# Bidirectional GLA/pool hybrid block: weights one lead further ahead in the units, loads moved up, attention put later into r

## The chip, the cores and the metric

One NeuronCore of a Trainium2 chip runs the whole kernel in one launch. The metric is device time in microseconds (us), the median of several runs; the profile is of one further execution of the same program. The engines are TensorE (PE in the profile; PEld is its loading of weights), VectorE (DVE), ScalarE (ACT), GpSimd (POOL) and SyncE (SP), from whose one queue nearly all DMAs are issued, in the order of the program.

## The reference

One layer of a hybrid encoder on x of 1024 tokens by 1024 features, float32:

```python
h = rmsnorm(x, norm_mix[l])
proj = h @ w_in[l]
q, k, v, r, lr_f, lr_b, u, g_a, g_b = jnp.split(proj, split_points, axis=-1)
# widths 512, 512, 1024, 1024, 16, 16, 512, 1024, 1024
log_a_f = jax.nn.log_sigmoid(lr_f @ w_decay_up_fwd[l] + b_decay_fwd[l]) / 16    # and log_a_b
o = gla_chunked(q, k, v, log_a_f, True) + flipped gla_chunked(..., log_a_b, False)   # 4 heads
o = o * lax.rsqrt(jnp.mean(o * o, axis=-1, keepdims=True) + EPS)
o = o * gla_norm[l] * jax.nn.silu(r)
y_a = o @ w_branch_gla[l]
y_b = (grouped linear map of multiscale_pool(u)) * pool_scale[l]      # windows 2, 4, 8, 16
merged = jax.nn.sigmoid(g_a) * y_a + jax.nn.sigmoid(g_b) * y_b
x = x + merged @ w_out[l]
h2 = rmsnorm(x, norm_ffn[l])
gate, up = jnp.split(h2 @ w_ffn_in[l], 2, axis=-1)                    # 2816 each
x = x + (jax.nn.silu(gate) * up) @ w_ffn_out[l]
return rmsnorm(x, norm_final)
```

## The kernel before

**Products.** Every float32 operand is split into a high and a low part (`split_to`: a cast on ScalarE, L197, gives hi; a subtraction, L198, on VectorE or for weights on GpSimd, gives lo). A product is three matmuls (hi hi, hi lo, lo hi; `mm3`, with the matmul in L269). Matmuls are of 128 x 128 weights on 512 columns. Many of the projections are made in two-by-two blocks by a scheme with seven products instead of eight (p = 1 to 7), whose combined operands VectorE and GpSimd prepare.

**The order of work.** The program is written in the order in which TensorE is to run, and each engine runs its own instructions in the order written. Side work is woven in by `pump`, called after every `mm3` with 1 (a "pump" is three matmuls): it runs things put off, weights in the making (`pending`), jobs beside (`aside`, each job charging so many pumps, from `prepare_beside`), and generators at the side (`side`, from `begin(generator, delay in pumps)`, each `yield` saying how many pumps to wait). `finish_beside` runs out what remains of the jobs at that place.

**The stages**, in order:

1. Norms, transposition to feature-major hT, and the values of head 0 (`values`, called for t = 0 to 6 in steps of two); `low_rank_weights` at t == 4. Then v of head 0 and half of hT are stored (`flush` issues what `later` deferred).
2. The decays' low-rank product (lrT, cast in L962, subtraction in L963), then `project_qk`: q and k of head 0, whose weights come through `fetch` (issue the load of raw weights, L205), `prepare` and `take`, in the order of `order`. Beside it run `feature_jobs`: sums of blocks of hT on VectorE (hs, L588), cast to trh (L582) and its rest trl (L573). They charge `SUMS` pumps each. `first_unit` is called by `project_qk` at each half of q and k.
3. Sixteen units (`gate_units`): two for u, three for the q and k of heads 1 to 3, three for v, four each for the gates a and b. A unit makes two column blocks of 128 by seven products of 12 matmuls. Its raw weights (fraw, two loads of 512 KB in `Unit.load`, L850) are combined (`Unit.source`, fs, L858), cast (wh) and reduced (wl, on GpSimd). `gates_ahead.step()` does this for the next product in the sequence of all units; one step is called in the loop ahead of each product, and some are called ahead of the loop. The pool `wts` has six buffers for wh and wl, four for raw and fs; the pool `slots` has 39 buffers of 512 KB. At the side run `decays`, then `pooling`.
4. r: eight projections of 16 `mm3`s, 128 pumps in all, over h (hh, hl); half of hT is read back from `h_out`. At the side runs `attention(h)` for the four heads: keys transposed (kp, L833, cast to kt), states (kv), outputs (op), normalized in L822, transposed (tp, L1399) and gated with r. Beside it run `branch_jobs` and `output_jobs`, sums of weights of the two coming projections on GpSimd (wsum, L588), stored to `s_out` and `t_wo` (L569).
5. `project(BRANCH)` and the merged projection, each of seven products with pieces from `line`: `line_load` (wraw, L1032), `line_sums`, `line_make` (casts and splits of weights wh, wl and data dh, dl). `load_block` (ob, L1060) reads back gated attention outputs.
6. The feed-forward part, untouched by the change.

The three constants that the change meets are `AHEAD = 4`, `SLOTS = 39` and `READY = 2`.

Of the kernel before, what the change touches and what calls it, by code (L numbers as in the profile page):

```python
# [11 lines left out]
F32R = mybir.dt.float32r  # L12
# [8 lines left out]
KT = D // P  # L21
# [21 lines left out]
AHEAD = 4  # L43
# [8 lines left out]
def kernel(  # L52
# [20 lines left out]
    nc = tc.nc  # L73
# [17 lines left out]
    def name(s):  # L91
        count[0] += 1
        return f"{s}_{count[0]}"

    def slot(dtype=F32, shape=(2, HALF), s="slot"):
        return slots.tile([P, *shape], dtype, tag="slot", name=name(s))
# [13 lines left out]
    def as_f32(ap):  # L110
        return ap.bitcast(F32)
# [74 lines left out]
    def begin(gen, delay=0.0):  # L186
        side.append([gen, delay])
# [12 lines left out]
    def load(src, kts, c0, width):  # L200
        per = min(HALF // width, kts)
        tiles = []
        for k0 in range(0, kts, per):
            raw = wts.tile([P, per, width], F32, tag="raw", name=name("raw"), bufs=4)
            nc.sync.dma_start(  # L205
                raw[:, :, :],
                src[k0 * P : (k0 + per) * P, c0 : c0 + width].rearrange("(k p) c -> p k c", p=P),
            )
            tiles.append(raw)
        return tiles  # L210
# [30 lines left out]
    def fetch():  # L241
        src = next(order, None)
        if src is not None:
            loaded.append(load(*src))

    def prepare():
        if not loaded:
            fetch()
        if loaded:
            ready.append(Weights(loaded.pop(0)))  # L250

            credit[0] = -2.0
# [101 lines left out]
    def load_up(i, d, w):  # L354
        r = 2 * RANK * i + RANK * d
        nc.sync.dma_start(uraw[r : r + RANK, :, d, :], w[0].rearrange("r (h c) -> r h c", h=HEADS))
# [12 lines left out]
    hT = Activations("h")  # L369
# [7 lines left out]
    def norms(t0):  # L377
        for t in (t0, t0 + 1):
            norm_x(t)
            yield 2  # L380
# [13 lines left out]
    def low_rank_weights():  # L394
        for i in range(2):
            raw = lraw[:, 4 * i : 4 * i + 4, :]
            nc.scalar.copy(lw[i][:, :, :3, :], raw.unsqueeze(2).broadcast_to([P, 4, 3, 2 * RANK]))
            nc.vector.tensor_tensor(lw[i][:, :, 3, :], raw, as_f32(lw[i][:, :, 0, :]), op=ALU.subtract)
        nc.scalar.copy(up[:, :, :, :], uraw[:, :, :, :])
        nc.vector.tensor_tensor(up[32:64], uraw[32:64], as_f32(up[32:64]), op=ALU.subtract)  # L400

    def value_slots():
        return [(slot(F32R, (4, DV), "vh"), slot(F32R, (4, DV), "vl")) for _ in range(2)]

    v = value_slots()
    v_out = [[dram.tile([P, NT, DV], F32, name=f"v_out{h}{n}") for n in range(2)] for h in range(HEADS)]
    qk_out = [[dram.tile([P, 2, HALF], F32, name=f"qk_out{h}{n}") for n in range(2)] for h in range(HEADS)]
    h_out = [[dram.tile([P, 2, HALF], F32, name=f"h_out{kp}{n}") for n in range(2)] for kp in range(2)]
# [24 lines left out]
    for t in range(0, NT, 2):  # L433
        if t + 4 < NT:
            begin(norms(t + 4), 1)
        if t == 2:
            for d, w_up in enumerate((w_decay_up_fwd, w_decay_up_bwd)):
                for i in range(4):
                    load_up(i, d, w_up)
        values(w, v, t)  # L440
        finish_side()
        if t + 2 < NT:
            begin(to_features(xn[(t + 2) % 4 :], t + 2, hT, g_mix), 0.5)
        values(w, v, t + 1)
        finish_side()
        if t == 4:
            low_rank_weights()
    deferred = []

# [3 lines left out]
    def flush(eng=nc.sync):  # L453
        while deferred:
            eng.dma_start(*deferred.pop(0))
# [140 lines left out]
    def prepare_beside(jobs, every, put=PUT, lag=1):  # L596
        aside.append([beside(chain(*jobs), every, put, lag), every])

    def finish_beside():
        while aside:  # L600
            for _ in aside[0][0]:
                pass
            aside.pop(0)
# [86 lines left out]
    def load_values(h, half):  # L690
        parts = v_heads.setdefault(h, {})[half] = [slot(F32R, (4, DV), s) for s in ("vh", "vl")]
        for n, t in enumerate(parts):
            nc.sync.dma_start(as_f32(t[:, :, :]), v_out[h][n][:, 4 * half : 4 * half + 4, :])

    def apply_decay(h, half, d):
        q, k, qe, ke = heads[h]
# [236 lines left out]
    kinds = [("u", i) for i in range(2)] + [("q", h) for h in range(1, HEADS)] + [("v", h) for h in range(1, HEADS)]  # L933
# [10 lines left out]
    gunits = [Unit(w_in, cols) for cols in gate_units]  # L944
# [1 line left out]
    gate_runs[-1] = last_run(len(gate_units) - 1)  # L946
    gates_ahead = Ahead(gunits, chain(*(steps_of(n, n == len(gate_units) - 1) for n in range(len(gate_units)))))

    SUMS = 2.1
    prepare_beside([feature_jobs(0), feature_jobs(1)], SUMS)  # L950
    prepare()
    lrT = slot(F32R, (2, HALF), "lrT")
# [9 lines left out]
        nc.scalar.copy(lrT[:, half, :], ps[:, :])  # L962
        nc.vector.tensor_tensor(lrT[64:96, half, :], ps[64:96, :], as_f32(lrT[64:96, half, :]), op=ALU.subtract)  # L963
    def first_unit(k, half):
        if k and half == 0:
            for _ in range(2):
                gunits[0].load()
        elif k:
            gates_ahead.step()

    project_qk(first_unit)
    finish_beside()
    for _ in range(AHEAD - 3):
        gates_ahead.step()
    flush()
    for p, i, half in ((1, 0, 0), (2, 1, 0), (3, 1, 1)):
        right[p] = [hT.pair(2 * i + c, half) for c in range(2)]

# [32 lines left out]
    line, loads, made, begun_sums = [], [], [], []  # L1011

    def line_load():
        if len(loads) < len(line):
            loads.append(line[len(loads)][0]())

    def line_sums():
        if len(begun_sums) < len(line):
            begun_sums.append(line[len(begun_sums)][1]())

    def line_make():
        n = len(made)
        if n < len(line):
            while len(loads) <= n:
                line_load()
            while len(begun_sums) <= n:
                line_sums()
            made.append(line[n][2](loads[n]))
# [25 lines left out]
    ob = {}  # L1054

    def load_block(i, j):

        ob[i, j] = [slot(s="ob") for _ in range(2)]
        for c in range(2):
            nc.sync.dma_start(ob[i, j][c][:, :, :], ob_out[i, 1 - j][:, 2 * c : 2 * c + 2, :])  # L1060
# [118 lines left out]
    def finish_late():  # L1179
        while late:  # L1180
            late.pop(0)()
# [86 lines left out]
    for n, run in enumerate(gate_runs):  # L1268
        zs[n] = Gates(n)
        last = n == len(gate_units) - 1  # L1270
        if n == FIRST_B + 1:
            finish_side()
            finish_beside()
            prepare_beside(map(unit_jobs, range(READY)), 3.1, 1, 2)
        if last:
            finish_beside()
        for at, (of, p) in enumerate(run):
            gates_ahead.step()
            zs[of].run(p)
            if p in (7, 4):  # L1280
                zs[of].store(int(p == 4))
            if at == 3:
                flush()
            for _ in range(2 * (at == 3 and not last)):
                gunits[n + 1].load()
            if n == 2 and at == 4:
                begin(pooling(), 4)
            if FIRST_B - 1 <= n < FIRST_B + 3 and at == 5:
                load_pool_weights(n - FIRST_B + 1)
            elif n >= FIRST_B and at == 2:  # L1290
                split_pool_weights(n - FIRST_B)
            if n >= FIRST_B and at == (0 if last else 3):
                load_pooled(n - FIRST_B)
            if last and at == 1:
                fetch()
                load_head(0)
            elif last and at == 4:
                load_values(0, 1)
                load_values(0, 0)
                prepare()  # L1300
    finish_late()
    flush()
    right.clear()

# [81 lines left out]
            nc.sync.dma_start(x2[t][:, :], x[t * P : (t + 1) * P, :])  # L1386

    mm_banks = cycle([ps_mm])
    for kp in range(2):
        hT.tiles[kp, 1] = tuple(slot(F32R, s="h" + s) for s in "hl")  # L1390
        for n, t in enumerate(hT.tiles[kp, 1]):
            nc.sync.dma_start(as_f32(t[:, :, :]), h_out[kp][n])
    oT, silu_r = {}, []

    def gated(j, half, sr):
# [30 lines left out]
            put_by()  # L1426

    for h in range(HEADS):
        begin(attention(h))
    prepare_beside(chain(map(branch_jobs, range(4)), map(output_jobs, range(4))), 3)  # L1430
    for j in range(KT):
        w = take()
        r = slot(s="r")
        for half in range(2):
            ps = feature_major(w, hT, half)
            flush()
            nc.scalar.activation(r[:, half, :], ps[:, :], AF.Silu)
            silu_r.append((j, half, r[:, half, :]))
            for _ in range(2):
                put_by()  # L1440
            if j == KT - 1:
                if half == 0:
                    finish_beside()
                    load_block(0, 0)
                    line_load()
                    line_load()
                else:
                    load_block(0, 1)
    finish_beside()
    u2, v2 = ([slot(s="sum") for _ in range(2)] for _ in range(2))  # L1450
    project(0, BRANCH, collect_branch, before_branch)

# [395 lines left out]
    for at, p in enumerate(OUT_ORDER):  # L1848
# [4 lines left out]
        for i in range(CLOSE if closing else n_of):  # L1853
            n = at * n_of + i
# [50 lines left out]
```

## Time and profile before

| | us |
|---|---|
| median of 3 runs | 1516.45 |
| lowest, highest | 1516.37, 1517.91 |
| the profiled execution, its own time | 1518.15 |
| its span, first to last instruction | 1516.4 |
| TensorE busy | 1399.6 (92%) |
| VectorE, ScalarE, GpSimd busy | 881.5, 649.5, 768.9 |

The span is what the profile's rows add up in; the time of an execution is a little longer. Stage 2 runs from 45 us, the first product on sums of hT starts at 94.66, the last unit's products end and r begins at 472.06, r's last transposition ends at 674.67, the branch projection begins at 689.43. The mean granted clock of TensorE is 0.970 of full speed.

A row of the waits says which engine, tile and line waited for which, in all, how often and longest. "Busy" is time in which an engine runs instructions; idle time of an engine that does not set the end costs nothing.

### The profile page before, as it was taken

The numbers are of one execution on the slowest core, as the hardware profiler recorded it, in microseconds if no ns is written. First come the engines' busy times: TensorE is split into PE (matmuls) and PEld (weight loads), VectorE is DVE, ScalarE is ACT, GpSimd is POOL, SyncE is SP. The second block draws the span as 40 slices with busy tenths as digits, with TensorE's granted clock in tenths as the row PEclk, the third lists the DMA queues.
The fourth block names the chain that finished last, engine by engine and source line by source line (L and its number), as shares of the span: only waits on it lengthen the run. The fifth ranks groups of instructions, "written<-read, shape, count | busy, mean of one in ns | idle before, by whom it ended". The sixth has DMA issues, their size and how long they took to land.

```text
span 1516.4 us, 18227 instructions
## 1 busy us (share of the span) xinstructions
PE 1399.6 (92%) x6365; PEld 1145.4 (76%) x6365; DVE 881.5 (58%) x1103; ACT 649.5 (43%) x1138; POOL 768.9 (51%) x576
## 2 busy tenths in 40 slices
PE   7868899989987999977999899999999999999997
PEld 6756677767766888756777688888888888888876
DVE  6584556567462676746676577555555555553353
ACT  6255566644442444314424653333333333453243
POOL 2234444444554352446556516666666667555344
PEclk9989999999998999988999999999999999999999
DMA  5413453655798675449551456445445445886451
GB/s 178 139 61 120 125 165 113 205 177 165 251 325 301 202 257 204 151 142 357 188 189 41 151 187 218 160 160 160 160 160 160 160 160 199 290 318 228 156 216 71
DMA packets 182588, 279.26 MB, mean 184 GB/s; under 512 B 12088, under 2 KB 102240, under 8 KB 182496
## 3 DMA queue, kind: packets, MB, share of 16 engines
q1 hardware_dynamic: 182496, 278.10, 53.9%
q8 instruction: 50, 0.82, 0.2%
q14 instruction: 42, 0.34, 0.1%
HBM read 182.37 MB, written 95.68 MB: 183 GB/s over the span
## 4 chain that ended last, share of the span: by engine, by line
PE 49%; issue 5%; POOL 4%; DVE 4%; DMA 3%; ACT 1%; SPq 0%; POOLq 0%; DVEq 0%; ACTq 0%
PE ps L269 47%; POOL wsum L588 1%; POOL wl L198 1%; DMA wsum<-in_w_out_dram 1%; DVE res L1798 1%; DMA ke<-dec_out 1%; DMA wor<-t_out 1%; DVE dl L162 0%; DMA wraw<-in_w_branch_gla_dram 0%; PE tr L1512 0%; POOL qe L698 0%; PE kv L269 0%; DVE xn L305 0%; DMA wsum<-in_w_branch_gla_dram 0%; POOL n3rs L1564 0%
## 5 line engine op out<-in xcount | busy, mean ns | idle before, releaser
L198 POOL TENSOR_TENSOR wl<-fs,wh 128x512 fp32r<-128x512 f32 x144 | 201.1, 1400 | 225.3 <-ACT wh L197 197.1
L269 PE MATMUL ps<-gh,wh 128*128 128x512 f32 x616 | 240.4, 390 | 0.0
L269 PE MATMUL ps<-gh,wl 128*128 128x512 f32 x616 | 239.7, 389 | 0.0
L269 PE MATMUL ps<-gl,wh 128*128 128x512 f32 x616 | 239.6, 389 | 0.0
L198 POOL TENSOR_TENSOR wl<-fraw,wh 128x512 fp32r<-128x512 f32 x108 | 153.1, 1417 | 120.5 <-ACT wh L197 97.9
L269 PE MATMUL ps<-hh,wh 128*128 128x512 f32 x352 | 149.3, 424 | 9.4 <-ACT wh L197 9.3
L198 POOL TENSOR_TENSOR ol<-gor,oh 128x1024 fp32r<-128x1024 f32 (+1 forms) x42 | 100.3, 2395 | 94.5 <-ACT oh L197 79.0
L269 PE MATMUL ps<-hh,wl 128*128 128x512 f32 x352 | 141.6, 402 | 3.7 <-POOL wl L198 2.9
L269 PE MATMUL ps<-hl,wh 128*128 128x512 f32 x352 | 140.9, 400 | 0.0
L269 PEld LDWEIGHTS ps<-gh,wl 128*128 128x128 f32 x616 | 115.6, 188 | 24.0
L269 PEld LDWEIGHTS ps<-gl,wh 128*128 128x128 f32 x616 | 115.6, 188 | 23.9
L269 PEld LDWEIGHTS ps<-gh,wh 128*128 128x128 f32 x616 | 115.6, 188 | 23.7
L269 PE MATMUL ps<-oh,oh 128*128 128x512 f32 x308 | 120.0, 390 | 2.5 <-DVE x L1827 2.5
L269 PE MATMUL ps<-trh,wh 128*128 128x512 f32 x256 | 103.4, 404 | 18.6 <-ACT wh L197 18.6
L269 PE MATMUL ps<-ol,oh 128*128 128x512 f32 x308 | 119.9, 389 | 0.2 <-DVE ol L198 0.2
L269 PE MATMUL ps<-oh,ol 128*128 128x512 f32 x308 | 119.9, 389 | 0.0
L198 POOL TENSOR_TENSOR wl<-wraw,wh 128x512 fp32r<-128x512 f32 x56 | 90.0, 1636 | 55.9 <-ACT wh L197 55.9
L269 PE MATMUL ps<-trh,wl 128*128 128x512 f32 x256 | 104.8, 409 | 14.3 <-POOL wl L198 14.2
L269 PE MATMUL ps<-trl,wh 128*128 128x512 f32 x256 | 101.8, 398 | 0.0
L197 ACT CAST wh<-fs 128x512 fp32r<-128x512 f32 x144 | 88.4, 614 | 28.5 <-DVE fs L858 26.0
L198 DVE TENSOR_TENSOR ol<-wor,oh 128x1024 fp32r<-128x1024 f32 (+1 forms) x42 | 62.0, 1496 | 52.9 <-ACT oh L197 45.6
L198 POOL TENSOR_TENSOR wl<-raw,wh 128x512 fp32r<-128x512 f32 x23 | 32.5, 1426 | 114.1 <-ACT wh L197 110.6
(254 smaller groups left out, 3057.4 us busy)
## 6 DMA issues: line engine op xcount, KB each, us to landing
fraw<-in_w_ffn_in_dram SPq DMA_DIRECT2D x44, 512.0 KB, 6.1
gor<-g_out SPq DMA_DIRECT2D x35, 512.0 KB, 5.8
fraw<-in_w_in_dram SPq DMA_DIRECT2D x32, 512.0 KB, 6.8
g_out<-s SPq DMA_DIRECT2D x44, 256.0 KB, 2.3
wor<-t_out SPq DMA_DIRECT2D x20, 512.0 KB
g_out<-g SPq DMA_DIRECT2D x33, 256.0 KB, 2.6
x<-in_x_dram SPq DMA_DIRECT2D x16, 512.0 KB, 5.7
wor<-in_w_ffn_out_dram SPq DMA_DIRECT2D x15, 512.0 KB, 11.2
```

What stands on the lines that cost most here:

```text
L197: nc.scalar.copy(hi, src)
L198: eng.tensor_tensor(lo, src, as_f32(hi), op=ALU.subtract)
L269: nc.tensor.matmul(ps, a[i], b[j], start=first and n == 0, stop=last and n == 2, skip_group_check=onto)
L588: op()
L1798: nc.vector.scalar_tensor_tensor(res[:, COLS[j]], x2[t][:, COLS[j]], rs[:, :], gain_final[:, COLS[j]], op0=ALU.mult, op1=ALU.mult)
```

## The change

- Four steps of the units' weights, not two, are made ahead of the loop: `first_unit` takes a step at both halves of k, and two follow (`AHEAD - 2`).
- The raw loads of q and k are issued at t == 4, ahead of the stores of v and h.
- `SUMS` is 1.6 instead of 2.1; the first unit's raw loads go out ahead of `prepare_beside`; the `flush` behind `finish_beside` is dropped (q and k are stored with the next flush, in the first unit).
- The raw loads of the next unit go out at its predecessor's first product (third, when either is a v unit) instead of the fourth.
- In the last unit the loads of h come at the fifth product, r's second weights at the sixth, one half of head 0's values at the seventh and the other behind the loop.
- `attention(0)` begins eight pumps into r.
- Branch and output jobs charge 2 pumps instead of 3; their rest, two line loads and the loads of blocks (0, 0) and (0, 1) come 16 pumps ahead of r's end; a piece of the line is made behind each half of r's last projection, with `line_sums` held to one ahead of what is made and `line_make` to data that are there.

```diff
--- before.py
+++ after.py
@@ -444,6 +444,8 @@
         values(w, v, t + 1)
         finish_side()
         if t == 4:
+            for _ in range(2):
+                fetch()
             low_rank_weights()
     deferred = []
 
@@ -691,6 +693,12 @@
         parts = v_heads.setdefault(h, {})[half] = [slot(F32R, (4, DV), s) for s in ("vh", "vl")]
         for n, t in enumerate(parts):
             nc.sync.dma_start(as_f32(t[:, :, :]), v_out[h][n][:, 4 * half : 4 * half + 4, :])
+
+    def load_features():
+        for kp in range(2):
+            hT.tiles[kp, 1] = tuple(slot(F32R, s="h" + s) for s in "hl")
+            for n, t in enumerate(hT.tiles[kp, 1]):
+                nc.sync.dma_start(as_f32(t[:, :, :]), h_out[kp][n])
 
     def apply_decay(h, half, d):
         q, k, qe, ke = heads[h]
@@ -946,7 +954,9 @@
     gate_runs[-1] = last_run(len(gate_units) - 1)
     gates_ahead = Ahead(gunits, chain(*(steps_of(n, n == len(gate_units) - 1) for n in range(len(gate_units)))))
 
-    SUMS = 2.1
+    SUMS = 1.6
+    for _ in range(2):
+        gunits[0].load()
     prepare_beside([feature_jobs(0), feature_jobs(1)], SUMS)
     prepare()
     lrT = slot(F32R, (2, HALF), "lrT")
@@ -962,17 +972,13 @@
         nc.scalar.copy(lrT[:, half, :], ps[:, :])
         nc.vector.tensor_tensor(lrT[64:96, half, :], ps[64:96, :], as_f32(lrT[64:96, half, :]), op=ALU.subtract)
     def first_unit(k, half):
-        if k and half == 0:
-            for _ in range(2):
-                gunits[0].load()
-        elif k:
+        if k:
             gates_ahead.step()
 
     project_qk(first_unit)
     finish_beside()
-    for _ in range(AHEAD - 3):
+    for _ in range(AHEAD - 2):
         gates_ahead.step()
-    flush()
     for p, i, half in ((1, 0, 0), (2, 1, 0), (3, 1, 1)):
         right[p] = [hT.pair(2 * i + c, half) for c in range(2)]
 
@@ -1015,12 +1021,12 @@
             loads.append(line[len(loads)][0]())
 
     def line_sums():
-        if len(begun_sums) < len(line):
+        if len(begun_sums) < min(len(line), len(made) + 1):
             begun_sums.append(line[len(begun_sums)][1]())
 
     def line_make():
         n = len(made)
-        if n < len(line):
+        if n < len(line) and not (n // 2 == 1 and len(ob.get((1, 0), ())) <= n % 2):
             while len(loads) <= n:
                 line_load()
             while len(begun_sums) <= n:
@@ -1281,7 +1287,7 @@
                 zs[of].store(int(p == 4))
             if at == 3:
                 flush()
-            for _ in range(2 * (at == 3 and not last)):
+            for _ in range(2 * (at == (2 if "v" in (kinds[n][0], kinds[n - 1][0]) else 0) and not last)):
                 gunits[n + 1].load()
             if n == 2 and at == 4:
                 begin(pooling(), 4)
@@ -1295,10 +1301,13 @@
                 fetch()
                 load_head(0)
             elif last and at == 4:
+                load_features()
+            elif last and at == 5:
+                prepare()
+            elif last and at == 6:
                 load_values(0, 1)
-                load_values(0, 0)
-                prepare()
     finish_late()
+    load_values(0, 0)
     flush()
     right.clear()
 
@@ -1386,10 +1395,6 @@
             nc.sync.dma_start(x2[t][:, :], x[t * P : (t + 1) * P, :])
 
     mm_banks = cycle([ps_mm])
-    for kp in range(2):
-        hT.tiles[kp, 1] = tuple(slot(F32R, s="h" + s) for s in "hl")
-        for n, t in enumerate(hT.tiles[kp, 1]):
-            nc.sync.dma_start(as_f32(t[:, :, :]), h_out[kp][n])
     oT, silu_r = {}, []
 
     def gated(j, half, sr):
@@ -1426,8 +1431,8 @@
             put_by()
 
     for h in range(HEADS):
-        begin(attention(h))
-    prepare_beside(chain(map(branch_jobs, range(4)), map(output_jobs, range(4))), 3)
+        begin(attention(h), 0 if h else 8)
+    prepare_beside(chain(map(branch_jobs, range(4)), map(output_jobs, range(4))), 2)
     for j in range(KT):
         w = take()
         r = slot(s="r")
@@ -1438,15 +1443,14 @@
             silu_r.append((j, half, r[:, half, :]))
             for _ in range(2):
                 put_by()
-            if j == KT - 1:
-                if half == 0:
-                    finish_beside()
-                    load_block(0, 0)
-                    line_load()
-                    line_load()
-                else:
-                    load_block(0, 1)
-    finish_beside()
+            if (j, half) == (KT - 2, 1):
+                finish_beside()
+                line_load()
+                line_load()
+                load_block(0, 0)
+                load_block(0, 1)
+            elif j == KT - 1:
+                line_make()
     u2, v2 = ([slot(s="sum") for _ in range(2)] for _ in range(2))
     project(0, BRANCH, collect_branch, before_branch)
```

## The prediction

> **What bounds the kernel now.** I read the page first, then who TensorE waits for, then busy time by stretches, then the stretches in order of time. On the page TensorE (PE) is busy for 92% of the span, the next engine for 58%.
>
> ```profile
> span 1516.4 us, 18227 instructions
> ...
> PE 1399.6 (92%) x6365; PEld 1145.4 (76%) x6365; DVE 881.5 (58%) x1103; ACT 649.5 (43%) x1138; POOL 768.9 (51%) x576
> ```
>
> So TensorE bounds it, and the most that better overlap can give is its idle time, 1516.4 - 1399.6 = 116.8 us, plus what a reduced clock costs. The waits (microseconds in total, times, longest) name who holds it up:
>
> ```profile
> PE ps L269 <- ACT wh L197: 43.6, 13, 14.8
> PE ps L269 <- POOL wl L198: 20.2, 32, 1.3
> PE ps L269 <- DVE dl L162: 11.2, 5, 3.4
> ...
> PE tp L1399 <- DVE o L822: 3.9, 5, 1.0
> ```
>
> The first two are weights made too late. Busy time by stretches (microseconds, then PE with its instructions, PEld, DVE, ACT, POOL, granted clock, share of the DMA engines, GB/s) gives the rate and the clock:
>
> ```profile
> 94.66:472.06 377.40, 344.03 (x1443) 268.61 (x1444) 214.39 (x289) 200.61 (x351) 179.20 (x148) 0.97 0.55 182
> 1000.00:1200.00 200.00, 200.00 (x884) 165.58 (x884) 117.62 (x118) 70.28 (x126) 132.58 (x96) 1.00 0.51 165
> 90.33:100.57 10.24, 5.27 (x12) 3.69 (x13) 7.68 (x8) 4.59 (x8) 4.55 (x3) 0.50 0.53 154
> 114.23:121.06 6.83, 6.08 (x14) 4.35 (x15) 2.35 (x3) 1.02 (x3) 3.29 (x3) 0.50 0.45 171
> 168.84:172.25 3.41, 3.23 (x8) 2.55 (x9) 0.00 (x0) 0.00 (x0) 1.36 (x2) 0.50 0.50 199
> 447.50:485.50 38.00, 30.03 (x126) 24.16 (x125) 12.99 (x19) 8.28 (x15) 13.48 (x11) 0.92 0.93 330
> 448.73:452.14 3.41, 3.41 (x10) 2.62 (x9) 2.62 (x5) 0.62 (x1) 1.28 (x1) 0.50 1.00 300
> 482.87:493.11 10.24, 5.53 (x17) 4.58 (x18) 2.07 (x4) 4.70 (x7) 6.29 (x5) 0.50 0.69 221
> 663.77:670.60 6.83, 5.94 (x16) 4.65 (x17) 3.21 (x7) 0.00 (x0) 4.17 (x4) 0.50 0.80 267
> 677.43:694.50 17.07, 4.93 (x11) 3.31 (x12) 4.84 (x3) 5.12 (x7) 7.74 (x7) 0.50 0.89 321
> ```
>
> From 1000 to 1200 us a matmul goes every 200 / 884 = 0.2262 us. In seven of the short stretches the granted clock is 0.50. They lie around the long gaps and last some microseconds after work has resumed: such a gap costs its length and half of that tail. The changed program has the same matmuls, so whatever it gives must come from gaps and clock, and I go through them in order of time.
>
> **Part 1, the front (early load of q and k, faster sums).** Rows of the timeline (start, length, engine, line, operation, and in brackets the idle time before it with what ended it), of the queue, ScalarE, VectorE, then TensorE; each was asked for in its own short stretch:
>
> ```profile
> 51.31 4.00 SPq L205 DMA_DIRECT2D raw<-in_w_in_dram  x4
> 56.84 0.62 ACT L197 CAST wh<-raw 128x512 fp32r<-128x512 f32 x1 [10.97 <-DMA raw<-in_w_in_dram]
> 57.98 0.69 DVE L963 TENSOR_TENSOR lrT<-ps,lrT 32x512 fp32r<-32x512 f32 x1 [11.64 <-ACT lrT L962]
> 58.70 3.44 DVE L588 TENSOR_TENSOR hs<-hh,hl 128x1024 f32<-128x1024 f32 x2
> 91.78 1.22 DVE L588 TENSOR_TENSOR hs<-hs,hs 128x1024 f32<-128x1024 f32 x1
> 93.04 1.04 ACT L582 CAST trh<-hs 128x1024 fp32r<-128x1024 f32 x1 [3.45 <-DVE hs L588]
> 93.99 0.61 ACT L197 CAST wh<-fs 128x512 fp32r<-128x512 f32 x1
> 57.51 0.80 PE L269 MATMUL ps<-hh,wh 128*128 128x512 f32 x1 [4.77 <-ACT wh L197]
> 94.66 0.80 PE L269 MATMUL ps<-trh,wh 128*128 128x512 f32 x1 [9.29 <-ACT wh L197]
> ```
>
> The queue issues raw for q and k at 51.31, behind the stores; ScalarE stands 10.97 us for it, and behind that cast stands lrT's, and behind lrT the sums of features (hs) on VectorE. They fill VectorE from 58.70 until the last ends at 93.00, cast (trh) by 94.1; then comes one weight cast, then TensorE at 94.66. With the loads ahead of the stores the 4.77 us gap goes, but what ends last is the chain of sums, not TensorE: 34.3 us of VectorE work whose start moves from 58.70 to about 50.4 (lrT's last matmul is no longer behind raw), so its end moves to 84.7, the end of the cast to 85.8 and the first product, 0.6 us behind it as now, to about 86.8. The gain is 94.66 - 86.8 = 7.8 us, and the second gap remains, now about as long as before and with the same slow clock, since TensorE also finishes q and k earlier. SUMS 1.6 puts the jobs in earlier, but VectorE is already unbroken: nothing, though without the early start it would be this chain that stays. The two more steps made here put at most two 0.6 us casts and a combination ahead on ScalarE and VectorE; bounds 5 to 13 (the upper if the second gap falls below what lowers the clock). I take 7.8, nearest to the chain's own rows.
>
> **Part 2, the sixteen units (lead, loads at the unit's start).** From 94.66 to 472.06 there are 1443 PE instructions, of which 48 are short transposes:
>
> ```profile
> L1235 PE MATMUL vt<-ident,ga 128*128 128x128 f32 x48 | 6.7, 275 | 0.2
> ```
>
> 1395 x 0.2262 + at most 6.7 = 321 us of work in 377.4. The waits of that stretch are
>
> ```profile
> PE ps L269 <- POOL wl L198: 17.1, 26, 1.3
> PE ps L269 <- ACT wh L197: 13.9, 9, 3.1
> ```
>
> 31 us in 35 stalls, none over 3.1, besides 2 us of others and about 10 at half clock after 94.66 and in three shorter stretches; some 13 are spread too thin to be named. Two more steps ahead are two products of 12 matmuls, 2 x 2.7 = 5.4 us, more than the longest stall. The pool has six buffers of weights: five made ahead and the one of the product just done. A cast then waits for that product, whose end ScalarE waits for anyway with the eviction ahead of it: nothing. The loads must come sooner for this, since a step reads its raw weights 5.4 us earlier; at the start of a unit instead of at its fourth product they do, by three products or 8.1 us, and beside the v units by one. I take the 31 us and 7 of the clock's 10 (three of the four stretches; the one at 94.66 stays) as gone, and 2.6 of the rest: 40.6, stage 337. Bounds: 20 (below, as the first rival) and 46.
>
> **Part 3, the start of r.**
>
> ```profile
> 476.15 0.60 PE L833 MATMUL kp<-ident,ke 128*128 128x128 f32 x4
> 487.58 0.58 PE L269 MATMUL kv<-vh,kt 128*128 128x256 f32 x1 [9.43 <-ACT kt L197]
> 485.60 0.62 ACT L197 CAST wh<-raw 128x512 fp32r<-128x512 f32 x1 [14.12 <-DMA raw<-in_w_in_dram]
> 486.95 0.58 ACT L197 CAST kt<-kp 128x512 fp32r<-128x512 f32 x1
> ```
>
> Attention's first transposed keys kp are there at 476.7, but their cast stands on ScalarE behind two casts of weights whose raw lands at 485.5: it was issued behind head, values and h. Now h goes out at the last unit's fifth product, raw at the sixth and one half of the values at the seventh, and attention starts eight pumps (24 matmuls, 5.4 us) later: kp 9.5 us after r begins, kv at 11.4. By then some 9 MB have to land, counted from the issues: pooled features 1, raw twice 0.5, the head 3, h 2, values 1, rows of yb 1. At the 330 GB/s of 447.50:485.50 these take 27 us; they start 20 us ahead of r, so the last lands 7 us after it, before kv. The gap of 9.43 us goes, and 2.8 of the slow clock behind it (482.87:493.11, half of the 5.5 us that lie behind 487.58). I leave 3 of the 12.2 for late data (bounds 0 and 9.4; nearer to the lower, since the count is ahead by 4 us): 9.2. By the Trainium skill ("DMA: Bandwidth & Descriptors", Where 436 GB/s comes from) transfers between HBM and the core's memory stop at about 358 GB/s; the trace agrees, 330 at a busy share of 0.93 being 355. By that figure the 9 MB would take 25 us, an estimate, and the sum would have 1 us more.
>
> **Part 4, the end of r, and what lies beyond.**
>
> ```profile
> 671.00 9.62 SPq L569 DMA_DIRECT2D t_wo<-wsum  x6
> 681.70 0.90 SPq L1032 DMA_DIRECT2D wraw<-in_w_branch_gla_dram  x2
> 659.22 6.44 DVE L822 TENSOR_SCALAR o<-o,ors 128x256 f32<-128x256 f32 x8 [1.75 <-POOL ors L301]
> 689.43 0.79 PE L269 MATMUL ps<-dh,wh 128*128 128x512 f32 x1 [14.75 <-ACT wh L197]
> L822 DVE TENSOR_SCALAR o<-o,ors x32: 340/342/1469, 530.9 to 665.3; 128x256 f32<-128x256 f32 x32
> ```
>
> The first branch weights go out at 681.70, behind the stores of the last sums of the output weights, and TensorE stands 14.75 us for them. At two pumps a job instead of three the sums end by pump 112 of the 128 in r, and the loads of blocks and weights follow there, 154 matmuls or 35 us ahead of use. The gap goes; so does half of the 5.1 us of slow clock behind it (677.43:694.50; 2.5); so do the four tp waits at the last head, 3.3 of the 3.9 us in all, in which L822 runs beside GpSimd's sums, and 2.4 with them (663.77:670.60, half of the 4.8 behind 665.8). Sum 22.9. Late next: the cast of the scores behind those of dh and wh, which line_make now puts on ScalarE inside r (three of 0.6 us, 1.8), and a transposition that waits for head 3, which ends only at pump 122 (1.7). Left 19.4, bounds 14 and 23.
>
> Closer sums on GpSimd may meet L822 at the three other heads: between 0 and 3 x the 3.9 us that TensorE waited for it, 12; I take 6, as nothing tells the ends apart. The line of branch weights starts two made instead of none, which shortens the first of the later waits (ps L269 on DVE dl, 11.2 us in 5): between nothing and two of the five; I take 2. Together -4. The Trainium skill ("GPSIMD Engine Reference", Key points) says that GpSimd shares its SBUF interfaces with VectorE and contends with instructions that have two SBUF inputs or run in a two-port mode; it speaks against this part. The trace agrees as far as it goes: an L822 takes up to 1469 ns, beside the sums, where the median is 342 (the last row; shortest, median, longest). By that rule alone all three heads would pay, and the sum would be 6 us less.
>
> Together 7.8 + 40.6 + 9.2 + 19.4 - 4 = 73.0 us: the profiled execution of 1518.15 (span 1516.4 and 1.75 around it) would come to 1445.2. It stands 1.7 above the median of the runs, 1516.45, so the median goes to 1443.5.
>
> **The rivals.** *The lead is not what is short (first rival).* If GpSimd and ScalarE, with the decays beside them, make weights no faster than they are used, two more in stock are used up in the first units; the 26 waits for wl would stay (17.1), with a fourth of those for wh. For: there are many short waits of like length, as behind a chain that sets the pace. Against: in the 377 us GpSimd is busy 179 and ScalarE 201. Part 2 then gives 40.6 - 17.1 - 3.5 = 20.0, and the time is 1464.
>
> *The start of r waits for data.* Head, h, raw and values go through one queue, in order. For: DMA is busy 0.93 of that stretch already, and the units ahead end sooner. Against: the 4 us above. The 9.2 of part 3 go: 1453.
>
> *Slower: each unit waits for its raw weights.* The page's row of their issues
>
> ```profile
> fraw<-in_w_in_dram SPq DMA_DIRECT2D x32, 512.0 KB, 6.8
> ```
>
> gives 6.8 us to landing, and a lead of five reads them 5.4 us earlier. If slots for fraw come free only late in the unit before, the earlier issue is void, and as the queue is in order the stores behind it wait too. ScalarE, and behind it the evictions that TensorE's banks need, would stand up to 6.8 + 0.6 (a cast) = 7.4 us in each of 15 units, 111 us: 1443.5 + 111 = 1554. It is slower from 73 / 15 = 4.9 us a unit on. Against: in the order of the built program only the loads beside the v units have a slack (25 matmuls, 5.7 us) under the time to landing; the others have 47 and more.
>
> *It does nothing measurable:* the stalls would all have to come back behind another engine, which the idle shares speak against. 1516.
>
> **How the numbers follow.** Forecast 0.68, first rival 0.15, data at r 0.09, units waiting 0.05, nothing 0.03. Measurement can tell about 0.2% here, so faster 0.92, same 0.03, slower 0.05. The low end takes the upper bounds of the parts (13, 46, 12.2 and 23 less 4, 90 us: 1426); the high end takes the first rival and the second together (1516 - 73 + 20.6 + 9.4, 1473) and the full 12 of the GpSimd charge: 1480.
>
> **What would show it.** A trace in which PE ps <- ACT wh and <- POOL wl shrink to under 20 us, no gap over 5 us at the start of r and at its end, one of 9 to 10 that ends near 87, and the units taking 335 to 340 us bears it out. Waits on wl as many as before show the first rival; waits of ScalarE or VectorE on fraw in each unit the slower one.

## The result, and the profile after

The changed kernel takes 1466.55 us (median of 4, 1464.51 to 1468.01) against 1516.41 us (4, 1516.07 to 1517.91): a ratio of 0.9668, with a 95% interval of 0.9652 to 0.9685. It is faster by 50 us; 73 were forecast. The profiled execution took 1468.01 us with a span of 1466.3. Line numbers above 450 are shifted by two to ten against the kernel before (L822 is L830 here, L963 is L973). From the page and the waits of TensorE, the rows that answer to those of before:

```profile
span 1466.3 us, 18225 instructions
...
PE 1381.7 (94%) x6365; PEld 1145.0 (78%) x6365; DVE 886.8 (60%) x1103; ACT 647.4 (44%) x1138; POOL 768.9 (52%) x576
```

```profile
PE ps L269 <- DVE dl L162: 12.9, 6, 3.7
PE ps L269 <- ACT wh L197: 9.8, 2, 8.9
PE vt L1241 <- DVE ga L1215: 7.2, 2, 5.1
...
PE kv L269 <- ACT kt L197: 6.5, 2, 5.8
PE tp L1404 <- DVE o L830: 5.3, 4, 2.6
PE vt L1241 <- ACT ga L1222: 4.9, 2, 3.1
...
PE ps L269 <- POOL wl L198: 3.4, 6, 1.3
```

The waits for weights, 43.6 and 20.2 us before, are down to 9.8 and 3.4, and 8.9 of the 9.8 is the one gap at the first product on sums. New are waits of vt, the transpositions in the three v units. Waits for dl, the split data of the branch and merged projections, are 12.9 where they were 11.2. The stages in stretches (us, PE and its instructions, PEld, DVE, ACT, POOL, clock, DMA share, GB/s): the units, r up to the first branch product, the two projections behind it, and one stretch of slow clock:

```profile
86.06:436.57 350.51, 331.64 (x1444) 271.42 (x1445) 218.87 (x288) 199.84 (x352) 174.12 (x145) 0.98 0.60 196
436.57:639.24 202.67, 182.54 (x1010) 155.98 (x1008) 127.58 (x244) 75.93 (x180) 91.58 (x68) 0.96 0.71 247
639.24:805.05 165.81, 149.30 (x622) 119.33 (x622) 120.48 (x121) 65.56 (x105) 97.05 (x62) 0.95 0.45 155
...
548.27:558.51 10.24, 7.54 (x24) 5.69 (x24) 8.14 (x14) 1.50 (x3) 3.59 (x3) 0.50 0.66 219
```

| stage | before, us | after, us | gained |
|---|---|---|---|
| up to the first product on sums | 94.66 | 86.06 | 8.6 |
| the units | 377.40 | 350.51 | 26.9 |
| r, up to the first branch product | 217.37 | 202.67 | 14.7 |
| branch and merged projections | 164.4 | 165.8 | -1.4 |
| the rest | 662.6 | 661.2 | 1.4 |

The stages of before are cut at the same instructions. The forecast had 7.8, 40.6, and 24.6 for the next two together, where 13.3 came.

### The profile page after: what moved, and what is told of

It is laid out like the page before. It is cut to its first block, busy times and chain, and to the rows that moved or that the text cites. A ratio compares the mean times of both kernels' runs of the same rounds, so it can differ in the third digit from the quotient of the medians.

```text
span 1466.3 us, 18225 instructions
## 1 busy us (share of the span) xinstructions
PE 1381.7 (94%) x6365; PEld 1145.0 (78%) x6365; DVE 886.8 (60%) x1103; ACT 647.4 (44%) x1138; POOL 768.9 (52%) x576
## 4 chain that ended last, share of the span: by engine, by line
PE 68%; DVE 9%; issue 7%; DMA 6%; POOL 5%; ACT 4%; SPq 0%; POOLq 0%; DVEq 0%; ACTq 0%
PE ps L269 62%; POOL wl L198 2%; DMA raw<-in_w_in_dram 2%; DMA fraw<-in_w_in_dram 1%; DVE hs L590 1%; DMA pl<-p_out 1%; PE op L801 1%; POOL wsum L590 1%; PE kv L269 1%; DMA hh<-h_out 1%; PE sc L748 1%; ACT wh L197 1%; PE yb L269 1%; DVE fs L866 1%; PE tr L316 1%
## 5 line engine op out<-in xcount | busy, mean ns | idle before, releaser
L198 POOL TENSOR_TENSOR wl<-fs,wh 128x512 fp32r<-128x512 f32 x144 | 198.1, 1378 | 205.6 <-ACT wh L197 173.6
L269 PE MATMUL ps<-trh,wl 128*128 128x512 f32 x256 | 100.8, 394 | 0.2 <-POOL wl L198 0.2
## 6 DMA issues: line engine op xcount, KB each, us to landing
wor<-in_w_ffn_out_dram SPq DMA_DIRECT2D x15, 512.0 KB, 11.2
```

Source lines behind the costliest of these rows:

```text
L198: eng.tensor_tensor(lo, src, as_f32(hi), op=ALU.subtract)
L269: nc.tensor.matmul(ps, a[i], b[j], start=first and n == 0, stop=last and n == 2, skip_group_check=onto)
```

## The experiments

Theories. *Lead:* the two more steps of weights took the waits for weights away. Its rival is the prediction's first: the makers set the pace, and the time near 1464 is that. *Queue:* the shortfall in the units comes from raw loads that stand in the one queue behind stores that wait. *Order of the line:* the projections gained nothing because a piece of the line is made late. Each run changes the changed kernel (1466.55) as its diff shows.

**lead3: the old lead, all loads early.**

```diff
-        if k:
+        if k and half:
             gates_ahead.step()
-    for _ in range(AHEAD - 2):
+    for _ in range(AHEAD - 3):
```

> The changed kernel with the lead of before: one step of weights in project_qk and one behind it instead of two and two; all loads stay early. If the lead is what took the waits for weights away, they come back: PE ps waits for ACT wh and POOL wl in the units rise from 9.1 us (8.9 of it at the first product) to over 25, the units take 15 to 28 us longer, time 1482 to 1495. If the earlier raw loads took them away and the lead adds nothing, the time stays within 3 us of 1466.5.

Measured 1497.84 us (0.9875 of before, 0.986 to 0.9889), 2.8 past the end of what was expected: the lead is worth 31.3 us. In the units TensorE waits again for both halves of the weights:

```profile
PE ps L269 <- ACT wh L197: 15.1, 9, 3.2
PE ps L269 <- POOL wl L198: 15.0, 22, 1.5
```

These are the numbers of before (13.9 and 17.1), with early loads. So the makers could keep pace and were only asked too late: the first rival falls, although the measured time is near its number. In the profiled execution the units take 31.0 us longer, from 91.18 to 472.65, more than the 15 to 28 expected. Another 5.1 are lost ahead of them, since the first product on sums starts at 91.18 instead of 86.06, and the later stages give 8 back.

**nofetch: q's and k's weights loaded behind the stores again.**

```diff
         if t == 4:
-            for _ in range(2):
-                fetch()
             low_rank_weights()
```

> The changed kernel with q's and k's raw weights loaded where they were before, behind the stores. If the early load is what starts the chain of sums sooner, the first product on sums comes at 94 to 95 us again instead of 86: 1473 to 1476. If the other moves there (the first unit's loads, SUMS 1.6) do it, it stays at 86 to 88 and the time at 1466 to 1469.

Measured 1477.24 us (0.9735, 0.9719 to 0.9752), 10.7 more. The first product on sums starts at

```profile
98.37 0.80 PE L269 MATMUL ps<-trh,wh 128*128 128x512 f32 x1 [9.36 <-ACT wh L197]
```

12.3 us later than with the fetch, and 3.7 later than in the kernel before. So without the early load the other moves at the front gain nothing and cost a little. The load does not carry the gain alone either: lead3 has it, and starts at 91.18. The start comes 3.4 us after the expected 94 to 95, and the time is 1.2 us past its range.

**dec_act: the decays' stores from ScalarE's queue. load0: the unit's loads at the first product beside the v units too.**

```diff
-                        nc.sync.dma_start(dec_out[h][half][n][:, d, :], t[:, :])
+                        nc.scalar.dma_start(dec_out[h][half][n][:, d, :], t[:, :])
```

```diff
-            for _ in range(2 * (at == (2 if "v" in (kinds[n][0], kinds[n - 1][0]) else 0) and not last)):
+            for _ in range(2 * (at == 0 and not last)):
```

> The changed kernel with the decays' stores (dec_out) issued from ScalarE's queue instead of SyncE's. If raw weights come late beside the v units because their loads stand in the queue behind these stores, which wait for the decays, then VectorE's wait of 16 us for fraw from 190 to 280 shrinks to under 5 and the four gaps ahead of vt (12.1 us) with about 3 of slow clock go: 1452 to 1458, less what 32 issues cost ScalarE. If the loads wait for a free slot, the waits and the time stay.

> The changed kernel with the raw loads of the next unit at the first product also beside the v units (there it is the third). If it is the distance of the load that is short, two products (5.4 us) take most of the fs waits (9.3, and about 3.5 each) and of the vt gaps: 1454 to 1460. If the queue stands behind the decays' stores wherever the load is put among them, the loads go out when they do now and the time stays at 1463 to 1468.

dec_act took 1458.29 us (0.9617, 0.9601 to 0.9633), 8.3 less and 0.3 past the end of its range, which left out what the issues cost; load0 1455.87 us (0.9599, 0.9585 to 0.9614), 10.7 less and inside. The changed kernel's timeline shows what they took away; SyncE's queue first, then VectorE, then TensorE:

```profile
190.97 0.42 SPq L664 DMA_DIRECT2D dec_out<-la  x1
191.49 1.20 SPq L858 DMA_DIRECT2D fraw<-in_w_in_dram  x2
199.12 0.83 DVE L866 TENSOR_TENSOR fs<-fraw 128x512 f32<-128x512 f32 x1 [9.27 <-DMA fraw<-in_w_in_dram]
210.74 1.76 PE L1241 MATMUL vt<-ident,ga 128*128 128x128 f32 x7 [5.07 <-DVE ga L1215]
```

The load goes out directly behind the last store of decays. In load0 the load of the same weights goes out 20 us sooner, though its place was moved by 5.4 us of products only, for it now stands ahead of the waiting stores:

```profile
171.87 1.46 SPq L858 DMA_DIRECT2D fraw<-in_w_in_dram  x2
188.18 0.34 SPq L664 DMA_DIRECT2D dec_out<-cum  x1
```

In dec_act, where the stores stand in another queue, it goes out at 171.46. So the two runs agree on the queue, and load0's distance helps by passing the stores. In the changed kernel the queue's own waits from 180 to 282 us begin with these stores:

```profile
SPq L664 <- DVE cum L651: 50.1, 5, 14.3
SPq L664 <- ACT facs L658: 19.6, 8, 6.7
```

VectorE then stands 9.27 us for the raw weights. In its order stand, behind that, the decays and the sum ga of the unit's last product, and TensorE's transposition of that sum waits 5.07 us at 210.74. VectorE's waits for fraw between 190 and 280 are

```profile
DVE fs L866 <- DMA fraw<-in_w_in_dram: 16.3, 3, 9.3
```

in the changed kernel; neither dec_act nor load0 has any left there. In both, TensorE's waits at vt shrink but do not go: of 12.1 us, 7.7 (dec_act) and 5.1 (load0) remain. With load0 the units take 339.8 us, near the 337 that the prediction gave them.

**raw_first, load0_raw_ahead: r's raw weights further ahead.** The first fetches one projection's weights ahead of head 0's values; the second keeps that distance through r, on top of load0.

```diff
             elif last and at == 4:
                 load_features()
+                fetch()
```

```diff
         w = take()
+        fetch()          # load0_raw_ahead alone
```

> The changed kernel with one fetch more at the last unit's fifth product: the raw weights of r's second projection go out behind h and ahead of head 0's values and the last rows, instead of behind them. If the place in the queue makes kv wait (its keys' cast stands behind the cast of this raw), the gap of 5.8 us and some 2.8 of slow clock behind it go: 1457 to 1460. If it is the transfers' total that binds, the values come later by what raw comes sooner, kv waits for vh, and the time stays at 1465 to 1467.

> The changed kernel with the next unit's raw loads at the first product everywhere (1455.9 by itself) and r's raw weights fetched one projection further ahead all through r. Fetching one of them earlier by itself gave 1463.8: the gap at kv went and a gap of 5.0 us at the first op came, where ScalarE stood 10.9 us for the next raw, whose load had gone out behind the sums' stores. If that is the whole of the loss at the start of r, both gaps go, with some 3 us of slow clock: 1445 to 1449. If ScalarE then waits for the sums, the values or GpSimd's qe in the same place, 1451 to 1455.

Measured 1463.80 us (0.9649, 0.9635 to 0.9664), only 2.8 less and between its two ranges, and 1449.61 us (0.9556, 0.9538 to 0.9574), 6.3 less than load0 and 0.6 over what was expected. In the changed kernel the start of r reads, in the queue, on ScalarE and on TensorE:

```profile
435.66 0.32 SPq L695 DMA_DIRECT2D vl<-v_out  x1
436.95 1.79 SPq L457 DMA_DIRECT2D yb_out<-ga  x2
439.45 3.18 SPq L205 DMA_DIRECT2D raw<-in_w_in_dram  x2
449.95 0.62 ACT L197 CAST wh<-raw 128x512 fp32r<-128x512 f32 x1 [13.96 <-DMA raw<-in_w_in_dram]
453.25 0.58 ACT L197 CAST kt<-kp 128x512 fp32r<-128x512 f32 x1
453.88 0.58 PE L269 MATMUL kv<-vh,kt 128*128 128x256 f32 x1 [5.79 <-ACT kt L197]
```

The raw weights are the last in the queue, ScalarE stands for them, and the keys' cast stands behind. With raw_first that gap is gone, and the next raw weights, issued behind stores of sums, stop ScalarE in the same way 14 us later:

```profile
463.56 0.62 ACT L197 CAST wh<-raw 128x512 fp32r<-128x512 f32 x1 [10.93 <-DMA raw<-in_w_in_dram]
469.45 0.58 PE L269 MATMUL op<-vh,p 128*128 128x256 f32 x1 [4.96 <-ACT p L197]
```

The wait had moved by one projection. Both gaps are gone when the distance is kept; the most that is left in r are short waits for sf (6.3 us in 6).

**every3: three pumps a job again.**

```diff
-    prepare_beside(chain(map(branch_jobs, range(4)), map(output_jobs, range(4))), 2)
+    prepare_beside(chain(map(branch_jobs, range(4)), map(output_jobs, range(4))), 3)
```

> The changed kernel with branch and output jobs charging 3 pumps again; what is left of them is still run out at pump 112, with the loads behind it. If it is the closer sums that cost at the other heads (tp waits 5.3 us, four op waits on sf), those go, but some 19 jobs then stand ahead of the loads at pump 112: 1460 to 1466. If the sums cost nothing by being closer, the jobs run out late only delay the loads: 1466 to 1474, with the waits of tp at the last head.

Measured 1467.26 us (0.968, 0.9659 to 0.9701), inside the second range, but no difference to 1466.55 that can be told. The waits for sf rise from 4.4 to 9.1 us (one of 7.3), those of tp fall from 5.3 to 4.0; the profiled execution took 1472.14, 5 us more than the others, so that these may not be theirs. The run does not separate what closer sums cost from what sums run out in a heap cost.

**delay0, delay3: attention begun at r's start, or three pumps into it.**

```diff
-        begin(attention(h), 0 if h else 8)
+        begin(attention(h))                      # delay0; "0 if h else 3" for delay3
```

> The changed kernel with attention begun at r's start, without the eight pumps. If the raw weights' landing sets when kv can start, the gap at kv grows by the 5.4 us that the delay covered, to about 11: 1469 to 1473. If attention later in r has room to give this back, or head 3 then ends sooner ahead of the branch, the time stays within 2 us of 1466.5.

> The changed kernel with attention begun three pumps into r instead of eight (none gave 1435.4). In the order of the program head 3 then still comes too late for its last rows to be gated ahead of the branch, so the third piece of the line is refused at r's end, as with eight. If that order is what costs, branch and merged projections take 165 to 167 us as with eight, not the 140 of none, and the time is 1462 to 1469. If it is the delay itself, it goes with its length: 1445 to 1449.

delay0 missed by far, on the good side: 1435.41 us (0.9458, 0.9439 to 0.9477), 31.1 less. The gap at kv grew to 8.6 us, as it should, but the two projections behind r went from 165.8 to 139.8 us and r itself from 202.7 to 197.8:

```profile
632.70:772.50 139.80, 139.06 (x614) 114.80 (x613) 115.76 (x117) 67.38 (x106) 99.45 (x61) 1.00 0.53 178
```

TensorE is busy all through it, at full clock; its one wait there is 0.7 us for dl. In the changed kernel it waits 16.5 us in that stage, 12.9 of them for dl, and a clock of 0.95 costs some 8 more. The casts of the pieces' data (dh) show why. First the changed kernel, then delay0:

```profile
630.23 1.05 ACT L1053 CAST dh<-ob 128x1024 fp32r<-128x1024 f32 x1
638.13 1.04 ACT L1053 CAST dh<-ob 128x1024 fp32r<-128x1024 f32 x1
640.11 1.05 ACT L1053 CAST dh<-o 128x1024 fp32r<-128x1024 f32 x1
...
652.33 1.06 ACT L1053 CAST dh<-o 128x1024 fp32r<-128x1024 f32 x1 [1.29 <-DVE o L1411]
```

```profile
625.79 1.04 ACT L1053 CAST dh<-ob 128x1024 fp32r<-128x1024 f32 x1
632.57 1.04 ACT L1053 CAST dh<-ob 128x1024 fp32r<-128x1024 f32 x1
634.54 1.05 ACT L1053 CAST dh<-o 128x1024 fp32r<-128x1024 f32 x1
636.53 1.06 ACT L1053 CAST dh<-o 128x1024 fp32r<-128x1024 f32 x1
```

The projections begin at 639.24 and 632.70. With attention eight pumps later, head 3's last rows are gated only inside the branch projection, line_make finds the fourth piece's data missing and returns (the expectations of delay3 and heads_first call it the third, at r's end; by the program it is the fourth, in the first product). That piece's cast comes 12 us behind the third's, where it is 2 us in delay0. Since each turn of the projection makes one piece, the line stays one piece shorter for good, and dl is late at one product after another. delay3 is the test: its order at r's end is that of eight pumps, and it took 1463.97 us (0.9656, 0.964 to 0.9671) with 166.1 us in the projections, as with eight pumps. It is the order, not the length of the delay.

**heads_first: eight pumps, and head 3 gated ahead of the last line_make.**

```diff
             elif j == KT - 1:
+                if half:
+                    finish_heads()
                 line_make()
```

> The changed kernel, attention at eight pumps, with finish_heads called at r's end ahead of the last line_make, so that the data of the third and fourth piece are there and the line is made one further ahead. If the order is what costs, the branch and merged projections take 139 to 142 us and the time is 1437 to 1445, though head 3's transpositions now stand ahead of the branch. If the delay costs in another way, it stays at 1462 to 1469.

Measured 1441.30 us (0.9504, 0.949 to 0.9519), the projections 139.9 us. With the order mended, the projections are as short as in delay0. What is left to it, 5.9 us, lies in r (203.5 us against 197.8); whether the delay costs this or head 3's end, which now stands ahead of the branch, the run does not separate.

**best_d0, best_hf: load0 and the raw weights ahead, with either cure.** Both are made of the diffs above: no delay, or eight pumps with finish_heads.

> The changed kernel with attention at r's start (1435.4 alone), unit loads at the first product everywhere (10.7 us alone) and r's raw weights one projection further ahead (6.3 on top of that). If the three are separate, 1435.4 - 10.7 - 6.3 = 1418, or down to 1414 as the gap at kv is longer without the delay; if kv then waits for head 0's values and sums instead, 1422 to 1427.

> The same three with attention left at eight pumps and finish_heads ahead of the last line_make. If order alone decided the project stage, and the delay still covers kv's data, 1418 to 1426; it is under best_d0 if the delay is worth something at r's start, and over it if head 3's end now stands in front of the branch.

best_d0 takes 1419.42 us (0.936, 0.9341 to 0.9379): it beats both kernels, by 96 and 47 us. The three gains add up, to 1 us (1435.4 - 10.7 - 6.3 = 1418.4). best_hf takes 1426.13 us (0.941, 0.9395 to 0.9424), 0.1 past its range. The stages of best_d0:

```profile
84.12:424.60 340.48, 329.12 (x1443) 269.39 (x1444) 218.24 (x288) 199.44 (x352) 175.33 (x146) 0.98 0.62 202
424.60:614.30 189.70, 180.00 (x1018) 154.75 (x1016) 131.05 (x246) 75.41 (x179) 91.45 (x68) 0.98 0.76 262
614.30:754.10 139.80, 139.08 (x615) 114.87 (x613) 115.75 (x117) 67.69 (x106) 99.65 (x61) 1.00 0.53 178
```

Of the 6.7 us between the two, 6.6 lie in r (196.3 us in best_hf). Its waits for tp are 3.0 against 0.6 us and for sf 5.0 against 2.8; that these are the cause, by heads that meet other work, was not tested.

## Why the prediction was right, and where it was wrong

The sign, the place of most gains and the range were right. The sum was 23 us too large, and three steps failed in their mechanism: the loads beside the v units, the place of r's raw weights in the queue, and the line behind r. That the result lies inside the range is in part luck: the range is 54 us wide, and of the three only late data at the start of r had been put into its high end.

**Part 1** held: 7.8 forecast, 8.6 came, 0.7 of it from a shorter wait at the program's very first matmul. (Its own rows add up to 85.8 + 0.6 = 86.4, not 86.8, and to a gain of 8.3.) The chain of sums starts at 50.19 instead of 58.70, the second gap remains (8.91 us) and ends at 86.06, and nofetch shows that it takes the load. What it overlooked is that the two more steps, priced as a small loss here, are needed too: without them (lead3) the start is at 91.18.

**Part 2** was right in its mechanism and mis-sized, 40.6 against 26.9. The 31 us of waits for weights went to 0.2 behind the first product, as the lead was said to do. The failed step is that the loads beside the v units come early enough. I counted their distance in matmuls of the program; what decided was the store in front of them in the queue. Nine stalls of 18.7 us came, 12.1 of them at vt and 4.9 for pooled features that came late by DMA. The thin rest gave 10 us instead of the 2.6 taken: 350.5 less 322 of work (the prediction's 1395 x 0.2262 + 6.7, which it gives as 321), 18.7 of stalls and some 7.5 of slow clock (15 us at half clock) leaves 2, where the same sum left 12 before.

**Part 3** was wrong in one step, 9.2 against 3.6: the gap of 9.43 became one of 5.79. I let raw go out at the last unit's sixth product, because prepare was moved there. But prepare only splits the weights that have been loaded; the next fetch comes with r's first take, and so behind both halves of the values and the last rows; the list of the change has the same mistake. The count was short by one half of the values and one store of rows, 2 MB of 11, and the 4 us in hand became a wait of 5.8.

**Part 4** was right about r's end: no gap is left ahead of the branch. It failed behind it. "A transposition that waits for head 3 (1.7)" was right that head 3 is late, but no transposition waited there (its four waits for o all lie at 548 us): the guard in line_make refused a piece, and the line never caught up. The delay of eight pumps was credited with covering the data at r's start; the runs put its whole effect at 31 us lost, 26 of them in the projections.

**The rivals.** The first rival's number, 1464, is 2.5 us from the result, and its mechanism is false (lead3): the right sum can come from the wrong terms. The second happened in part. The slower one happened at the v units alone, for 12 us instead of 111, where its own condition (25 matmuls of slack) had pointed. The charge of 6 us for closer sums came at one of the three heads. There the eight L830 take 6.34 us beside GpSimd's sums, and TensorE's transpositions wait; at the other three heads GpSimd runs no sum beside them, and the eight take 2.2:

```profile
501.43 2.19 DVE L830 TENSOR_SCALAR o<-o,ors 128x256 f32<-128x256 f32 x8 [1.55 <-POOL ors L301]
546.65 6.34 DVE L830 TENSOR_SCALAR o<-o,ors 128x256 f32<-128x256 f32 x8 [1.55 <-POOL ors L301]
548.06 0.33 PE L1404 MATMUL tp<-ident,o 128*128 128x128 f32 x1 [2.59 <-DVE o L830]
549.40 0.99 PE L1404 MATMUL tp<-ident,o 128*128 128x128 f32 x3 [1.01 <-DVE o L830]
551.28 0.45 PE L1404 MATMUL tp<-ident,o 128*128 128x128 f32 x1 [0.89 <-DVE o L830]
552.53 1.00 PE L1404 MATMUL tp<-ident,o 128*128 128x128 f32 x3 [0.80 <-DVE o L830]
```

These 5.3 us, with slow clock behind them, replace the 3.3 at the last head of the kernel before. In delay0, with the sums as close, one head meets them too (its eight take 5.37 us) and no transposition waits there, so the price depends on where the sums fall; what decides this was not tested.

**The rules weighed.** By the Trainium skill, "DMA: Bandwidth & Descriptors" (Where 436 GB/s comes from), the traffic between HBM and the core's memory ends at about 358 GB/s a core, half of what the HBM gives two cores. The changed kernel, on one core, moves more for 20 us around the start of r:

```profile
420.00:440.00 20.00, 20.00 (x90) 16.55 (x89) 9.34 (x14) 6.04 (x11) 5.30 (x4) 1.00 1.03 379
```

The trace of before only seemed to agree; here reads and stores together reach 379 GB/s, and the measurement decides. The Trainium skill's rule on GpSimd's shared interfaces ("GPSIMD Engine Reference", Key points: contention with instructions that have two SBUF inputs or run in a two-port mode) agrees with an L830 of up to 1418 ns beside sums of weights (median 348), and with the one head above; that L830 runs in such a mode no trace here shows. By that rule alone the prediction had all three heads pay; only one met the sums.

## What to carry to other kernels

Where TensorE waits in many small stalls for operands that other engines have time to make, make them more steps ahead; then look which transfer stands behind a waiting store in the same queue, since distance counted in instructions says nothing about that. A guard that skips a step when data are late costs more than the one step if the loop makes just one per turn: compare the order at the end of a stage for each delay, not the length of the delay. Undo each part by itself even when the whole is faster, for a part that loses can hide behind parts that gain.

## What the runs showed of the hardware

The clock falls without a long gap. In the merged projection of the changed kernel two waits under 1 us came after matmuls without a break from 788 to 795 us, and 6.83 us at half clock followed:

```profile
796.03 0.51 PE L269 MATMUL ps<-wh,dh 128*128 128x512 f32 x1 [0.92 <-ACT wh L197]
797.38 0.76 PE L269 MATMUL ps<-wl,dh 128*128 128x512 f32 x1 [0.84 <-POOL wl L198]
797.45:804.28 6.83, 3.70 (x8) 2.62 (x9) 6.79 (x5) 2.09 (x3) 4.07 (x3) 0.50 0.29 112
```

At 548 us the four waits of 2.59, 1.01, 0.89 and 0.80 us, with transpositions between, gave 10.24 us (the row 548.27:558.51 above), and in the kernel before four of 0.23 to 1.01 gave 6.83. The prediction had priced slow clock only behind the long gaps and where it stood already; its rows at 114, 168 and 448 us, which it puts around the long gaps, follow waits of at most 3.1. In the two projections the clock is 0.95 with 16.5 us of waits, none over 3.7, and 1.00 throughout with the one of 0.7 in delay0. Over the whole program, with fewer waits both short and long, the mean granted clock rises from 0.970 (before) to 0.979 (after).
